# The MLP's first weights split in two by a casting DMA, a ScalarE negation and an accumulating DMA in ten chunks

## The chip, the core and the metric

The kernel runs on one core of one Trainium2 chip. The metric is the device time of one launch in microseconds, the median over timed runs. The engines are called PE (TensorE), DVE (VectorE), ACT (ScalarE), POOL (GpSimd) and SP (SyncE), as the profile does.

## What is computed

A decoder trunk of two layers on 1024 tokens of 1024 channels, all in float32. Layer 0 mixes tokens with a gated linear recurrence, layer 1 with causal windows; each mixer is followed by an MLP of 4096 hidden channels, and that MLP is where the change lies:

```python
def sq_relu_mlp(h, w1, w2):
    u = jax.nn.relu(jnp.einsum("bsd,df->bsf", h, w1))
    return jnp.einsum("bsf,fd->bsd", u * u, w2)

for i in range(DEPTH):
    ...
    h = modulate(rms_norm(x, norm_ffn_g[i]), sh_f, sc_f)
    x = x + gt_f[:, None, :] * sq_relu_mlp(h, ffn_w1[i], ffn_w2[i])
return rms_norm(x, final_norm_g)
```

The shifts, scales and gates (sh_f, sc_f, gt_f) come from the conditioning, a product of one vector with 12 matrices of 1024 x 1024.

## The kernel before

**Two parts of every operand.** PE multiplies float32r operands. To keep float32 accuracy each operand is held as two float32r parts, a high part (the value rounded) and a low part (what the rounding left). mm3 (lines 174 to 180) then issues three matmuls: high x high, high x low, low x high. A weight unit is loaded by SP as a raw float32 tile of 128 x 1024 (512 KB, load, line 97), then split_part (lines 168 to 172) makes the two parts of each half: ACT rounds the raw half into the high part, and DVE subtracts the high part from the raw half.

**The MLP** runs over eight chunks of 512 hidden channels. f1 makes a chunk's hidden channels: four units of w1 (128 hidden channels each), each used for both halves of the tokens, 24 matmuls per unit and half, so 192 matmuls. f2_fast then multiplies by w2 in four passes (r = 0 to 3), each of seven products (Winograd's form of Strassen's method, in the order 1, 5, 6, 3, 7, 2, 4) of six matmuls, so 168 matmuls. A chunk thus has 360 matmuls. In the program's rows the weights of a pass are four tiles: w_a11_a12 (products 1 and 2), w_a22_s1 (4 and 5), w_s2_s4 (3 and 6), w_s3 (7); the profile shortens them to w_a_a, w_a_s, w_s_s and w_s.

**After each product** of f2_fast the result is added into x. Products 5, 3, 2 and 4 are added by DVE straight from PSUM (line 770; 5 twice). Product 1 is copied by ACT (c1, line 789) and scaled by ACT; products 6 and 7 are added onto c1 by DVE (lines 800, 804), scaled by ACT (c, line 774) and added into x by POOL (line 779): one add for 1, one for 6, two for 7. Some of these adds go to the same blocks of x, so they are chained: DVE's add of product 3 waits for POOL's add of product 6, and DVE's add of product 4 for POOL's first add of product 7.

**What holds the order.** A tile framework arranges each engine's instructions into a fixed queue and puts in the semaphores. Three limits matter here. PE's results rotate through six PSUM banks, so a product can start only when the result six before it has been taken away. The split weights rotate through eight tiles of wpool; a unit of f1 takes two, a pass of f2_fast four, so the first two units of a chunk (u0, u1) take the tiles of pass 2 of the chunk before, and u2, u3 those of pass 3. Units are prepared one ahead (class Ahead, line 663). And the raw tiles (rawp, three buffers) serve w1, w2 and the 80 tiles of the conditioning's weights (mb, line 212), which are worked off by DVE (line 197, 1.2 us or more each), one per weight unit, during layer 0's MLP.

Of the kernel before, what the change touches and what calls it, by code (L numbers as in the profile page):

```python
# [10 lines left out]
F32 = mybir.dt.float32  # L11
# [4 lines left out]
P = 128  # L16
# [12 lines left out]
# Columns of the packed per-channel vectors, eight columns (one per block of channels) each.  # L29
# [13 lines left out]
def trunk_kernel(ctx, tc, xT, vecs, wmod, w_k, w_in, w_y, w_g, w_out, w_p, w1, w2, outT):  # L43
# [16 lines left out]
    class Blocks:  # L60
        """Eight blocks of channels of one half of the tokens, in two slots"""
# [41 lines left out]
    # The weights of the first products, in the order in which they are used: two blocks of rows  # L103
    # of six blocks of the input projection, and the conditioning's blocks of columns.
    mod_raw, k_raw = {}, []

    def piece(r, q, part):
        """Columns of a part of r, which is halved for the first two blocks of rows."""
        n = r.shape[-1] // (2 if q == 0 else 1)
        return part * n, part * n + n  # L110
# [29 lines left out]
    # silu(c) as a row on every partition  # L140
    cs = const.tile([P, NB], F32, name="cs")
    with tc.issue_after(S.activation(cs, vcol("c"), AF.Sigmoid).ins):
        # has the table of the first norm's square root loaded ahead of it
        S.activation(const.tile([P, 1], F32, name="early"), eps, AF.Sqrt)
# [3 lines left out]
    for n in range(2):  # L148
        ps = small_ps()
        # the columns of cs on diagonals, whose sums over the partitions are on every partition  # L150
# [9 lines left out]
    def split_unit(src, name, eng=None, drips=None):  # L160
        raw = load(src, name)
        drip(rate[0] if drips is None else drips)
        return [split_part(raw[:, c:c + H], f"{name}_{c}", eng) for c in (0, H)]

# [9 lines left out]
    def mm3(ps, unit, col, rh, rl, first, last):  # L174
        """ps += unit[:, col:col+128].T @ (rh + rl)"""
# [6 lines left out]
    def proj(unit, hh, hl):  # L182
        """One 128-row block of W.T @ h for one token half, K = 1024."""
# [11 lines left out]
    def mod_column(m, e, raw):  # L195
        """m[:, e] = raw @ cond"""
# [9 lines left out]
    def mod_steps():  # L206
        """The rest of the conditioning in small steps, taken between those of the other work."""
# [19 lines left out]
    def norm_scale(g, m, name):  # L227
        """g * (1 + scale)"""
# [5 lines left out]
    class SumSq:  # L234
        """Sums of squares of n tokens: up to three partial sums, added up by the tensor engine."""
# [19 lines left out]
    def rstd_bcast(ss, trace=None):  # L255
        """PSUM tile [P, n] with 1/sqrt(mean + eps) of every token on every partition."""
# [10 lines left out]
        # in two float32r parts on diagonals, whose sums over the partitions are on every partition  # L267
# [38 lines left out]
    # Six blocks of the input projection take the channels of the first half of the tokens  # L306
    # as the conditioning of each 128 of them is ready.
# [8 lines left out]
    def after(f, *args, **kw):  # L316
        """Issues behind what the last call on the same engine issued."""
# [7 lines left out]
    def column(dst, j, k, scale, first):  # L325
        """dst[:, k] = first + scale * (conditioning of channel block k)"""
# [16 lines left out]
    def prepare(q, part=0):  # L343
        """The float32r parts of the weights of two blocks of rows, or of one if q is 0"""
# [126 lines left out]
    # coefficient of the gate in log a: 8 * log_sigmoid(lambda)  # L471
# [17 lines left out]
    # log1p(z) = 2 s (1 + po)  # L489
# [11 lines left out]
    def gates(hd, unit, h):  # L501
        """RG-LRU of one head; its states take the place of its input."""
# [16 lines left out]
        for mi in range(2):  # L519
            b = 2 * hd + mi  # L520
            # a = exp(log a);  1 - a^2 = (1 + a^2) * tanh(-log a)
# [77 lines left out]
    # U[c]: the hidden channels of chunk c, in slots of two blocks each: (first or last two blocks,  # L599
    # half of the tokens), and the sums of them that the second product of the MLP takes  # L600
# [3 lines left out]
    def f1_block(unit, j, h, u, fast):  # L604
# [7 lines left out]
        def minus(a, n):  # L612
            """a less a block that is there in its two parts"""
# [15 lines left out]
        # for f2_fast the halves of the tokens change places  # L629
# [33 lines left out]
    class Ahead:  # L663
        """Units of weights, which are prepared one ahead of those in use"""
# [11 lines left out]
    # pieces of the conditioning by unit of a chunk of the MLP  # L676
    DRIPS = (1, 1, 1, 1, 1, 1, 1, 1)

    def f1_jobs(i, c, eng=None):
# [5 lines left out]
    def f1(i, c, halves, by_half=False, eng=None, side=iter(()), fast=False, ahead=None):  # L685
        """`side` is other work, a step of which is traced after each unit.

        `fast` is set where f2_fast takes the result: "in turn" if one half of the tokens is done before the other.
        """
# [22 lines left out]
    def f2_weights(i, c, r, eng=None):  # L712
        """The parts of blocks of rows r and r + 4 of W2.T for f2_fast, by the product that takes them"""
# [18 lines left out]
    def f2_weights_one(i, c, r, eng):  # L732
        """Those of f2_weights for the products that the first half of the tokens takes"""
# [12 lines left out]
    def f2_weights_two(i, c, r, eng):  # L746
        """The others"""
# [5 lines left out]
    def f2_fast(i, c, ahead, products=(1, 5, 6, 3, 7, 2, 4), side=iter(())):  # L753
        """The second product of the MLP by Winograd's form of Strassen's seven products.
# [358 lines left out]
```

## Time and profile before

| | |
|---|---|
| timed runs | 1795.46, 1798.42, 1798.61 us; median 1798.42 |
| span of the profiled execution | 1797.3 us (its own time is not listed beside the span; the median lies 1.1 us above it) |
| PE busy | 1718.5 us, 96% of the span |
| DVE busy | 1419.8 us, 79% |
| ACT busy | 913.7 us, 51% |
| POOL busy | 585.9 us, 33% |
| chain that ended last | PE 62%, DVE 22%, ACT 5%, issue 5%, DMA 4%, POOL 2% |

Busy time is an average over stages. The number to ask for in a stage is not who is busy but how long PE stands idle there, and which engine ends that idle time. In the stages of the change PE is almost never idle.

### The profile page before, as it was taken

The page shows a single profiled execution, that of the slowest core. Times are in us where ns is not written, and L with a number is a line of the kernel's source. Part 1 is how long each engine was busy: PE and PEld are TensorE (multiplying, and loading weights), DVE is VectorE, ACT ScalarE, POOL GpSimd, SP SyncE. Part 2 cuts the span into 40 slices and gives each one's busy share as a digit, 9 for nine tenths or more (in the row PEclk, how much of TensorE's full clock was granted, in tenths as well). Part 3 has the DMA queues.
Part 4 walks back from the last instruction along what each step waited for, and adds up shares of the span by engine and source line. Part 5 has one row for each costly group of instructions (what it writes and reads, how often), then busy time and mean ns, then how long its engine had stood idle before and what let it go on. Part 6 is the DMA issues. An engine that isn't in the chain of part 4 may idle for free.

```text
span 1797.3 us, 20872 instructions
## 1 busy us (share of the span) xinstructions
PE 1718.5 (96%) x7510; PEld 1405.2 (78%) x7510; DVE 1419.8 (79%) x2124; ACT 913.7 (51%) x1558; POOL 585.9 (33%) x434
## 2 busy tenths in 40 slices
PE   6899989989999999999999988999999999999997
PEld 4687768778788888888888766788887787878787
DVE  8997866678888889898876897958787878686836
ACT  4588884255454444545454464445444444545422
POOL 5323341242322414151324655511322324041403
PEclk8999989989999999999999988999999999999999
DMA  9223314521424233242213221231202111121202
GB/s 363 73 84 109 136 47 142 162 83 59 136 70 134 73 115 106 94 126 73 83 58 106 81 72 59 83 105 51 70 33 71 36 59 52 42 61 46 71 13 94
DMA packets 47479, 158.76 MB, mean 88 GB/s; under 512 B 5008, under 2 KB 7440, under 8 KB 47376
## 3 DMA queue, kind: packets, MB, share of 16 engines
q1 hardware_dynamic: 47376, 157.43, 26.9%
q8 instruction: 59, 0.97, 0.2%
q14 instruction: 44, 0.36, 0.1%
HBM read 153.21 MB, written 4.19 MB: 88 GB/s over the span
## 4 chain that ended last, share of the span: by engine, by line
PE 62%; DVE 22%; ACT 5%; issue 5%; DMA 4%; POOL 2%; DVEq 0%; SPq 0%; ACTq 0%; POOLq 0%
PE mm L178 20%; PE mm L179 20%; PE mm L180 20%; DMA mb<-in_wmod 3%; DVE mb L197 2%; DVE xa L770 1%; DVE mw L323 1%; POOL xa L779 1%; DVE pw L900 1%; DVE xb L770 1%; DVE xca L439 1%; PE sm L262 1%; DVE hl L291 1%; DVE w_a_s L171 1%; DVE xcb L439 1%
## 5 line engine op out<-in xcount | busy, mean ns | idle before, releaser
L178 PE MATMUL mm<-hh,w_w 128*128 128x512 f32 x1024 | 401.4, 392 | 0.9 <-DVE xa L770 0.9
L180 PE MATMUL mm<-hh,w_w 128*128 128x512 f32 x1024 | 400.9, 392 | 0.0
L179 PE MATMUL mm<-hl,w_w 128*128 128x512 f32 x1024 | 400.6, 391 | 0.0
L779 POOL TENSOR_TENSOR xb<-xb,c 128x512 f32<-128x512 f32 x104 | 150.4, 1446 | 632.1 <-ACT c L774 564.4
L178 PEld LDWEIGHTS mm<-hh,w_w 128*128 128x128 f32 x1024 | 193.5, 189 | 42.8 <-DVE xa L770 2.7
L180 PEld LDWEIGHTS mm<-hh,w_w 128*128 128x128 f32 x1024 | 193.6, 189 | 40.3
L179 PEld LDWEIGHTS mm<-hl,w_w 128*128 128x128 f32 x1024 | 193.5, 189 | 40.0
L779 POOL TENSOR_TENSOR xa<-xa,c 128x512 f32<-128x512 f32 x104 | 160.3, 1542 | 145.1 <-ACT c L774 145.1
L774 ACT ACTIVATE c<-c,mod 128x512 f32<-128x512 f32 x104 | 75.3, 724 | 209.7 <-DVE c L800 119.8
L197 DVE SCALAR_TENSOR_TENSOR mb<-mb,cond 128x1024 f32<-128x1024 f32 x80 | 113.8, 1423 | 55.2 <-DMA mb<-in_wmod 54.6
L620 ACT ACTIVATE relu<-mm 128x512 f32<-128x512 f32 x128 | 76.2, 595 | 152.4 <-PE mm L180 143.6
L170 ACT CAST w_w<-raw_w 128x512 fp32r<-128x512 f32 x192 | 113.5, 614 | 63.2 <-PE mm L180 50.6
L171 DVE TENSOR_TENSOR w_w<-raw_w,w_w 128x512 fp32r<-128x512 f32 x136 | 130.5, 967 | 16.8 <-ACT w_w L170 16.7
L770 DVE SCALAR_TENSOR_TENSOR xa<-mm,mod,xa 128x512 f32<-128x512 f32 x156 | 112.9, 741 | 16.6 <-POOL xa L779 16.6
L171 POOL TENSOR_TENSOR w_w<-raw_w,w_w 128x512 fp32r<-128x512 f32 x56 | 83.5, 1498 | 71.6 <-ACT w_w L170 62.6
L179 PE MATMUL mm<-u,w_w 128*128 128x512 f32 (+1 forms) x224 | 81.4, 363 | 1.7 <-DVE u L610 1.7
L178 PE MATMUL mm<-u,w_w 128*128 128x512 f32 (+1 forms) x224 | 80.8, 364 | 1.7 <-ACT u L609 1.7
L180 PE MATMUL mm<-u,w_w 128*128 128x512 f32 (+1 forms) x224 | 81.0, 362 | 0.0
L178 PE MATMUL mm<-u,w_a_a 128*128 128x512 f32 x200 | 79.1, 396 | 1.9 <-DVE xa L770 1.0
L610 DVE TENSOR_TENSOR u<-usq,u 128x512 fp32r<-128x512 f32 x102 | 72.9, 715 | 8.5 <-ACT u L609 7.5
L770 DVE SCALAR_TENSOR_TENSOR xb<-mm,mod,xb 128x512 f32<-128x512 f32 x104 | 77.0, 741 | 2.6 <-PE mm L180 2.2
L179 PE MATMUL mm<-u,w_a_a 128*128 128x512 f32 x200 | 78.0, 390 | 0.0
(332 smaller groups left out, 4078.3 us busy)
## 6 DMA issues: line engine op xcount, KB each, us to landing
raw_w<-in_w SPq DMA_DIRECT2D x148, 512.0 KB, 3.6
mb<-in_wmod SPq DMA_DIRECT2D x80, 512.0 KB, 3.6
mw<-in_wmod SPq DMA_DIRECT2D x16, 512.0 KB, 9.6
raw_in<-in_w_in SPq DMA_DIRECT2D x8, 512.0 KB, 3.7
raw_y<-in_w_y SPq DMA_DIRECT2D x8, 512.0 KB, 3.6
raw_o<-in_w_out SPq DMA_DIRECT2D x8, 512.0 KB, 3.7
outT<-o SPq DMA_DIRECT2D x12, 256.0 KB, 2.4
xa<-in_xT SPq DMA_DIRECT2D x4, 512.0 KB, 5.4
```

The lines of the kernel that those rows point to most:

```text
L170: S.copy(w[:, 0, 0:n], raw)
L171: (eng or V).tensor_sub(w[:, 1, 0:n], raw, w[:, 0, 0:n].bitcast(F32))
L178: PE.matmul(out=ps, lhsT=wh, rhs=rh, start=first, stop=False)
L179: PE.matmul(out=ps, lhsT=wh, rhs=rl, start=False, stop=False)
L180: PE.matmul(out=ps, lhsT=w[:, 1, c:c + P], rhs=rh, start=False, stop=last)
L197: V.scalar_tensor_tensor(raw, raw, 1.0, cond, op0=ALU.mult, op1=ALU.mult, accum_out=m[:, e:e + 1])
L439: V.scalar_tensor_tensor(o, xr[:, k:k + H], vcol(f"cw{k}", m), o, op0=ALU.mult, op1=ALU.add)
L610: eng.tensor_sub(u[n][:, 1, jj, :], src, u[n][:, 0, jj, :].bitcast(F32))
L620: S.activation(r, ps, AF.Relu)
L770: V.scalar_tensor_tensor(xb, ps, g[:, r + 4 * row:r + 4 * row + 1], xb, op0=ALU.mult, op1=ALU.add)
L774: S.activation(t, src, AF.Identity, scale=g[:, r + 4 * row:r + 4 * row + 1])
L779: G.tensor_add(xb, xb, t)
```

## The change

In chunks 1 to 5 of layer 0 and 2 to 6 of layer 1 (ten chunks, 40 units, 80 halves) split_unit is replaced by dma_unit. For each half POOL issues a DMA that reads w1 from HBM and writes it cast to float32r into the high part; ACT writes the negated high part into the low part; POOL issues a second DMA that reads the same half of w1 again and adds it onto the low part. No raw tile, no load on SP, no ACT cast and no DVE subtraction are left for these units. Comments and docstrings go too, which changes nothing but line numbers.

```diff
+    def dma_unit(src, name, drips):
+        unit = [split_tile(f"{name}_{c}") for c in (0, H)]
+        for w, c in zip(unit, (0, H)):
+            nc.gpsimd.dma_start(w[:, 0, :], src[:, c:c + H])
+        drip(drips)
+        for w, c in zip(unit, (0, H)):
+            S.activation(w[:, 1, :], w[:, 0, :].bitcast(F32), AF.Identity, scale=-1.0)
+            nc.gpsimd.dma_start(w[:, 1, :], src[:, c:c + H], accum_op=ALU.add)
+        return unit
...
-    def f1_jobs(i, c, eng=None):
+    def f1_jobs(i, c, eng=None, by_dma=False):
+        if by_dma and eng is None:
+            return [partial(lambda j: dma_unit(w1[i, c * 4 + j], f"w1_{i}_{c}_{j}", DRIPS[j]), j) for j in range(4)]
...
         for c in range(first, last):
-            yield from f1_jobs(i, c, G if (i, c) == (0, 0) else None)
+            yield from f1_jobs(i, c, G if (i, c) == (0, 0) else None, c > first)
             yield from f2_jobs(i, c)
```

The scheduler places the new instructions. On POOL, late in layer 1's chunk 4 (pass 2's adds, then pass 3's first), this stood there before: the two adds xb_1_84 and xa_1_82 with c_12090 are those of product 7 of pass 2.

```order
L779 TENSOR_TENSOR xb_0_83<-xb_0_83,c_12051 128x512
L779 TENSOR_TENSOR xa_0_81<-xa_0_81,c_12071 128x512
L779 TENSOR_TENSOR xb_1_84<-xb_1_84,c_12090 128x512
L779 TENSOR_TENSOR xa_1_82<-xa_1_82,c_12090 128x512
L779 TENSOR_TENSOR xb_0_83<-xb_0_83,c_12127 128x512
```

The same place on POOL now; w_w1_1_5_0_0 is the first half of u0 of chunk 5, w_w1_1_5_0_512 its second, w_w1_1_5_1_0 the first of u1, line 169 the casting DMA and line 173 the accumulating one.

```order
L792 TENSOR_TENSOR xb_0_83<-xb_0_83,c_12051 128x512
L169 DMA w_w1_1_5_0_0_12110<-in_w1 128x512
L792 TENSOR_TENSOR xa_0_81<-xa_0_81,c_12071 128x512
L169 DMA w_w1_1_5_0_512_12111<-in_w1 128x512
L169 DMA w_w1_1_5_1_0_12193<-in_w1 128x512
L173 DMA w_w1_1_5_0_0_12110<-in_w1 128x512
L792 TENSOR_TENSOR xb_1_84<-xb_1_84,c_12090 128x512
L792 TENSOR_TENSOR xa_1_82<-xa_1_82,c_12090 128x512
L173 DMA w_w1_1_5_0_512_12111<-in_w1 128x512
L169 DMA w_w1_1_5_1_512_12194<-in_w1 128x512
L173 DMA w_w1_1_5_1_0_12193<-in_w1 128x512
L792 TENSOR_TENSOR xb_0_83<-xb_0_83,c_12127 128x512
```

Four DMAs have come ahead of product 7's adds, three of them between them and product 6's. In layer 0 the accumulating DMA of u0's first half stands behind both adds of product 7 and not ahead of them; the rest is alike.

On DVE at the same place there stood, from the last weight tile of pass 3 on:

```order
L171 TENSOR_TENSOR w_s3_12039<-raw_w2_1_4_3_12024,w_s3_12039 128x256
L770 SCALAR_TENSOR_TENSOR xa_0_81<-mm_12054,mod1_5_6290,xa_0_81 128x512
L770 SCALAR_TENSOR_TENSOR xa_1_82<-mm_12054,mod1_5_6290,xa_1_82 128x512
L800 TENSOR_TENSOR c1_12049<-mm_12063,c1_12049 128x512
L171 TENSOR_TENSOR w_w1_1_5_0_0_12112<-raw_w1_1_5_0_12110,w_w1_1_5_0_0_12112 128x512
L770 SCALAR_TENSOR_TENSOR xa_0_81<-mm_12074,mod1_5_6290,xa_0_81 128x512
L804 TENSOR_TENSOR c1_12049<-mm_12082,c1_12049 128x512
L171 TENSOR_TENSOR w_w1_1_5_0_512_12115<-raw_w1_1_5_0_12110,w_w1_1_5_0_512_12115 128x512
```

and now stand:

```order
L182 TENSOR_TENSOR w_s3_12039<-raw_w2_1_4_3_12024,w_s3_12039 128x256
L732 TENSOR_TENSOR raw_w2_1_5_1_12511<-raw_w2_1_5_1_12511 128x256
L734 TENSOR_TENSOR raw_w2_1_5_1_12511<-raw_w2_1_5_1_12511 128x256
L783 SCALAR_TENSOR_TENSOR xa_0_81<-mm_12054,mod1_5_6292,xa_0_81 128x512
L783 SCALAR_TENSOR_TENSOR xa_1_82<-mm_12054,mod1_5_6292,xa_1_82 128x512
L813 TENSOR_TENSOR c1_12049<-mm_12063,c1_12049 128x512
L732 TENSOR_TENSOR raw_w2_1_5_2_12597<-raw_w2_1_5_2_12597 128x256
L734 TENSOR_TENSOR raw_w2_1_5_2_12597<-raw_w2_1_5_2_12597 128x256
L783 SCALAR_TENSOR_TENSOR xa_0_81<-mm_12074,mod1_5_6292,xa_0_81 128x512
L817 TENSOR_TENSOR c1_12049<-mm_12082,c1_12049 128x512
```

The subtractions of w1 are gone, and preparations of the next chunk's w2 (lines 732, 734; raw tiles are free earlier) have moved up ahead of pass 2's evictions.

On ACT at the same place there now stand, with line 172 the negation:

```order
L787 ACTIVATE c_12071<-c1_12049,mod1_5_6292 128x512
L172 ACTIVATE w_w1_1_5_0_0_12110<-w_w1_1_5_0_0_12110 128x512
L787 ACTIVATE c_12090<-c1_12049,mod1_5_6292 128x512
L172 ACTIVATE w_w1_1_5_0_512_12111<-w_w1_1_5_0_512_12111 128x512
L172 ACTIVATE w_w1_1_5_1_0_12193<-w_w1_1_5_1_0_12193 128x512
L802 COPY c1_12125<-mm_12118 128x512
L787 ACTIVATE c_12127<-mm_12118,mod1_5_6292 128x512
```

Before, casts of the same halves stood in about these places. A cast waited for a raw tile that had been loaded long before; a negation waits for a DMA that POOL has just issued, and the copy and the scaling of product 1 of pass 3, which free its PSUM bank, queue behind it.

## Rows read from the trace of the kernel before

**Rows 1.** The page, part 1: busy time, share, instructions.
```profile
PE 1718.5 (96%) x7510; PEld 1405.2 (78%) x7510; DVE 1419.8 (79%) x2124; ACT 913.7 (51%) x1558; POOL 585.9 (33%) x434
```

**Rows 2.** Windows over five chunks of each layer: PE, PEld, DVE, ACT, POOL busy.
```profile
466.37:877.38 411.01, 410.24 (x1800) 337.58 (x1801) 354.45 (x558) 199.03 (x350) 125.34 (x80) 1.00 0.32 102
1277.97:1694.09 416.12, 411.08 (x1802) 337.24 (x1800) 325.50 (x470) 197.56 (x350) 113.10 (x80) 1.00 0.16 51
```

**Rows 3.** Timeline of PE: first matmuls of chunks, and three late ones.
```profile
466.37 0.50 PE L178 MATMUL mm<-hh,w_w 128*128 128x512 f32 x1 [0.92 <-DVE xa L770]
...
713.40 0.50 PE L178 MATMUL mm<-hh,w_w 128*128 128x512 f32 x1
...
792.70 0.50 PE L178 MATMUL mm<-u,w_a_a 128*128 128x512 f32 x1
...
795.64 0.50 PE L178 MATMUL mm<-hh,w_w 128*128 128x512 f32 x1
...
877.38 0.39 PE L178 MATMUL mm<-hh,w_w 128*128 128x512 f32 x1
...
1444.42 0.39 PE L178 MATMUL mm<-hh,w_w 128*128 128x512 f32 x1
...
1520.66 0.50 PE L178 MATMUL mm<-ut,w_s_s 128*128 128x512 f32 x1 [0.96 <-DVE xa L770]
...
1527.63 0.39 PE L178 MATMUL mm<-hh,w_w 128*128 128x512 f32 x1
```

**Rows 4.** Page, part 5: the two groups of which 80 instructions each go.
```profile
L170 ACT CAST w_w<-raw_w 128x512 fp32r<-128x512 f32 x192 | 113.5, 614 | 63.2 <-PE mm L180 50.6
L171 DVE TENSOR_TENSOR w_w<-raw_w,w_w 128x512 fp32r<-128x512 f32 x136 | 130.5, 967 | 16.8 <-ACT w_w L170 16.7
```

**Rows 5.** DMA issues: KB each, median us to landing; SP's own row.
```profile
raw_w<-in_w SPq DMA_DIRECT2D x148, 512.0 KB, 3.6
...
outT<-o SPq DMA_DIRECT2D x12, 256.0 KB, 2.4
...
xb<-in_xT SPq DMA_DIRECT2D x4, 512.0 KB, 6.7
...
743.13 0.33 SPq L715 DMA_DIRECT2D raw_w<-in_w  x1
```

**Rows 6.** Timeline of POOL, layer 1's chunk 4.
```profile
1518.11 1.29 POOL L779 TENSOR_TENSOR xa<-xa,c 128x512 f32<-128x512 f32 x1 [3.10 <-ACT c L774]
1522.10 1.30 POOL L779 TENSOR_TENSOR xb<-xb,c 128x512 f32<-128x512 f32 x1 [2.70 <-ACT c L774]
1523.35 1.75 POOL L779 TENSOR_TENSOR xa<-xa,c 128x512 f32<-128x512 f32 x1
```

**Rows 7.** Timeline of DVE, layer 1's chunk 4.
```profile
1515.22 1.40 DVE L770 SCALAR_TENSOR_TENSOR xa<-mm,mod,xa 128x512 f32<-128x512 f32 x2
1516.54 0.68 DVE L800 TENSOR_TENSOR c<-mm,c 128x512 f32<-128x512 f32 x1
1518.57 1.37 DVE L171 TENSOR_TENSOR w_w<-raw_w,w_w 128x512 fp32r<-128x512 f32 x1 [1.36 <-ACT w_w L170]
1519.87 0.74 DVE L770 SCALAR_TENSOR_TENSOR xa<-mm,mod,xa 128x512 f32<-128x512 f32 x1
```

**Rows 8.** Timeline of ACT, layer 1's chunk 4: the scalings of products 6, 7.
```profile
1517.31 0.72 ACT L774 ACTIVATE c<-c,mod 128x512 f32<-128x512 f32 x1 [3.67 <-DVE c L800]
...
1521.30 0.72 ACT L774 ACTIVATE c<-c,mod 128x512 f32<-128x512 f32 x1 [1.72 <-DVE c L804]
```

**Rows 9.** Timeline of DVE, layer 0's chunk 4.
```profile
784.76 0.67 DVE L800 TENSOR_TENSOR c<-mm,c 128x512 f32<-128x512 f32 x1
...
789.65 2.32 DVE L197 SCALAR_TENSOR_TENSOR mb<-mb,cond 128x1024 f32<-128x1024 f32 x1
...
791.90 0.74 DVE L770 SCALAR_TENSOR_TENSOR xb<-mm,mod,xb 128x512 f32<-128x512 f32 x1
...
794.19 1.40 DVE L770 SCALAR_TENSOR_TENSOR xa<-mm,mod,xa 128x512 f32<-128x512 f32 x2
```

**Rows 10.** Timeline of POOL, layer 0's chunk 4.
```profile
786.34 1.29 POOL L779 TENSOR_TENSOR xa<-xa,c 128x512 f32<-128x512 f32 x1 [4.24 <-ACT c L774]
```

## The prediction

> **What bounds the kernel now.** I read the page's busy part first: PE is busy 96% of the span, DVE 79%, POOL 33% [rows 1]. A share over the whole span says nothing of a stage, so next come the windows over the two stretches in which the ten changed chunks lie. There PE is busy 410.24 of 411.01 us in layer 0 and 411.08 of 416.12 us in layer 1 [rows 2]; the granted clock is 1.00 in both, the upper of its two levels. The reader is to see that PE has almost nothing to give back. DVE, from which the change takes work, is busy 354.45 and 325.50 us there: loaded, but not the engine that sets the pace.
>
> The timeline of PE says how much there is to win. The chunk that begins at 795.64 ends at 877.38 without a gap: 81.74 us for 360 matmuls, 0.227 us each and 1.36 us for a product of six. Layer 0's chunk before it takes 795.64 - 713.40 = 82.24 us, so 0.5 us are idle; layer 1's takes 1527.63 - 1444.42 = 83.21 us, so 1.47 us are idle [rows 3]. The rows name the cause: PE waits for DVE's line 770, the instruction that takes a result out of a PSUM bank. The gaps lie late in f2_fast, where DVE runs behind, and are alike in four chunks of each layer; one of about 2 us stands before 466.37, none before layer 1's first changed chunk. Ceiling of any gain: 2 + 4 x 0.5 + 4 x 1.47 = about 10 us.
>
> **What goes.** 80 casts on ACT (0.614 us) and 80 subtractions on DVE (0.967 us) [rows 4], 49 us and 77 us of busy time, and 40 loads on SP. ACT gets 80 negations for its 80 casts, the same shape at the same 0.61 us, so nothing net. Of DVE's 77 us only what frees a bank earlier counts, at most the 10 us above. The order shows that it does not free it early: the subtractions stood after the addition of product 6 in pass 2, and that is the start of the chain on which PE waits, while two preparations of w2 now stand ahead of it.
>
> **What comes.** 160 DMAs on POOL, 16 in a chunk, which did not issue a DMA before. Two prices are unknown. **The issue**, time in which POOL does nothing else: SP's own row is 0.33 us, a POOL instruction of this width takes 1.29 us and up to 1.75 us beside DVE [rows 5, 6]. I take 1.3 us, because it is POOL that must write the transfer out; ends 0.33 and 1.75. **The landing**, from the start of the issue: 256 KB land in 2.4 us from SP, 512 KB in 3.6 us, and in 6.7 us when the queues are full [rows 5]. I take 3.6 us, since the accumulating transfer moves its 256 KB in twice; ends 2.4 and 6.7. Below nothing neither can be. The second reading of w1 adds 21 MB; the DMA share of these stretches is 0.32 and 0.16 [rows 2], so I cost that traffic at nothing, under cover of idle transfer engines; if they were full the landing would be that of the 6.7 us row.
>
> The Trainium skill, DMA: Bandwidth & Descriptors (Anatomy of one DMA, GpSimd path), gives a fixed 2.0 us plus the bytes over 436 GB/s, an estimate of 2.6 us for 256 KB. No row here shows a POOL transfer; by that figure the sum below would be 4.5 us instead of 6.5.
>
> **Layer 1, one chunk end (chunk 4 into 5).** Before, DVE evicts product 5 of pass 2 at 1515.22, adds product 6 at 1516.54 [rows 7], ACT scales it at 1517.31 [rows 8], POOL adds it at 1518.11 [rows 6], and DVE's eviction of product 3 at 1519.87 frees the bank for PE at 1520.66 [rows 3]. Now lines 732 and 734 stand ahead of 1515.22; they are half as wide as the addition of 0.68 us [rows 7], and I take 0.4 us each, so 0.8 us. The chain shifts: product 6's scaling ends near 1518.8, POOL's add runs 1518.8 to 1520.1, DVE follows at once (before, it stood 0.5 us behind a 1.37 us subtraction), PE resumes at 1521.0, 0.3 us late, and would reach product 2, three products on, at 1525.1.
>
> Then POOL: two casting issues and the accumulating one, 3 x 1.3 us, bring it to 1524.0. Its operand for product 7 is there by 1522.4 (0.74 + 0.67 us on DVE and 0.72 us on ACT behind 1520.1); before, POOL took it at 1522.10 [rows 6]. The add ends at 1525.3, DVE's eviction of product 4 of pass 2, chained to it (0.74 us), at 1526.1, and product 2 of pass 3, which needs that bank, starts 1.0 us late. f1 starts 0.3 + 1.0 = **1.3 us later** than before. ACT's negations wait for the landings at 1520.1 + 3.6 and 1521.4 + 3.6 us; behind them the scaling of product 1 of pass 3 ends at 1526.9, and its bank is wanted at 1527.5: hidden by 0.6 us. The low part of u0's second half lands at 1526.9 + 3.6 = 1530.5, wanted at 1532: hidden.
> Ends: issue 0.33, landing 2.4: +0.3 us. Issue 1.75: three issues more by 0.45, +2.7 us. Landing 6.7: the last negation ends at 1528.7, the bank comes at 1530.0, +3.8 us.
>
> **Layer 0, one chunk end (chunk 4 into 5).** A conditioning tile on DVE (mb) has moved behind product 6's addition, so that addition comes some 1.2 us before 784.76 [rows 9]. POOL: casting issue to 785.7 (its tile is free at about 784.4: 795.64 less the gap and eight products), product 6's add to 787.0 (before: 786.34 to 787.63 [rows 10]), two casting issues to 789.6, the adds of product 7 to 790.9 and 792.5. DVE evicts product 4 by 791.7; before, it began at 791.90 behind a 2.32 us mb [rows 9], and PE's product 2 started at 792.70 [rows 3]. Now it starts at 792.4: 0.3 us won. Behind an mb of 1.2 and a line 732 of 0.4 us product 5 of pass 3 is evicted by 794.7 (before by 794.19 + 1.40 [rows 9]), f1 could start at 795.25. But the low part of u0's first half is issued at 792.5 and lands at 796.1; f1's third matmul wants it at 795.7. **Net 0.0 us**: the new wait eats what DVE gives. Behind ACT's negations the bank of product 1 comes at 793.8, as wanted.
> Ends: both low: -0.4 us. Issue 1.75: the low part lands at 797.45, +1.4 us. Landing 6.7: ACT's queue holds product 1's bank to 796.9, +3.1 us.
>
> u1, u2 and u3 have 11, 22 and 33 us more, which cover them in all these cases. ACT's negations for u2 and u3 stand ahead of f1's first relu and can hold it some 7 us; six banks of 5.4 us each cover that, and ACT, busy half of these stretches [rows 2], catches up within f1.
>
> **Sum.** 5 x 0.0 + 5 x 1.3 = +6.5 us. The profiled span of 1797.3 us becomes 1803.8; the median of the runs stands 1.1 us above the span, so 1798.42 + 6.5 = 1805 us. Ends: issue and landing low, 5 x (-0.4) + 5 x 0.3 = -0.5 us; issue 1.75, 5 x 1.4 + 5 x 2.7 = +20.5 us; landing 6.7, 5 x 3.1 + 5 x 3.8 = +34.5 us.
>
> **Rivals.**
> *Faster.* DVE's relief frees banks before the new queue hurts: POOL's issues are as short as SP's row, and the preparations of w2 that moved up fall into time in which DVE would wait anyway (1.36 us of idle stands in rows 7). Then half of the 10 us comes back: 1793 us. For it: every gap is PE waiting on DVE. Against: the gap's chain runs through ACT and POOL, both made later. It decides at an issue below about 0.5 us.
> *Nothing.* Issue between, chain shifts and relief cancel: 1798 us. For it: the reserves found above are small in both directions.
> *Much slower.* The landing is nearer 6.7 us or the issue 1.75 us or more: 1819 to 1833 us. For the issue: POOL's add of 1.30 us at 1522.10 became 1.75 us at 1523.35 beside DVE's work [rows 6], and DVE is busy 78% to 86% of these stretches. For the landing: ACT, in order, holds PSUM banks while it waits, which the casts did not.
> The Trainium skill, SBUF — State Buffer (SBUF: two separate sides), says that a DMA issued from POOL cannot get its descriptors written while DVE runs a two-port operation. The adds and subtractions here have two inputs and are not of that kind, so the rule as written would not bite; no row here shows an issue beside DVE.
> That the DMAs are not issued as described can be ruled out: the order shows them on POOL.
>
> **Chances.** The runs lie within 3.2 us, so 0.2%, 3.6 us, is what a measurement can tell from no change. Forecast (a few us slower, 1802 to 1813) 0.40; much slower 0.21; nothing 0.24; faster 0.15. That gives slower 0.61, same 0.24, faster 0.15. The range must leave out no more than 2 in 10: 1795 (below it only the faster case) to 1832 (the landing's end); on the slow side alone it is 1802 to 1832.
>
> **What would show it.** Right: PE's idle time in layer 1's changed chunks grows from 1.47 to about 2.8 us and now stands before products 2 and 4 of pass 3; in layer 0 it sits on f1's third matmul, with a DMA as releaser; POOL's issues take about 1.3 us, the landing about 3.6. The first matmuls of f1 in the chunk rows shift accordingly. Wrong: no waits on DMA or ACT at the chunk ends (faster or nothing), waits of over 2 us there in every chunk (much slower), or PE waiting inside f1, for u1 to u3, which I have costed at nothing.

## The result and the profile after

The changed kernel takes 1810.9 us (median of 4 runs, 1808.15 to 1812.79) against 1798.35 us (4 runs): ratio 1.0074, 95% interval 1.0059 to 1.0089. It is 12.5 us slower. The forecast said 1805 us, a few us slower. The time came out near it; the place where the prediction put the loss did not.

The page's first part, which answers to [rows 1]: DVE is 79 us less busy, POOL 100 us more, and PE has as much to do as before.

```profile
PE 1717.6 (95%) x7510; PEld 1404.1 (78%) x7510; DVE 1340.9 (74%) x2044; ACT 916.8 (51%) x1558; POOL 685.7 (38%) x594
```

The windows over the five chunks of each layer answer to [rows 2] (from, to, length, then PE, PEld, DVE, ACT, POOL busy, granted clock, DMA share, GB/s).

```profile
468.63:892.31 423.68, 411.93 (x1802) 336.42 (x1800) 327.25 (x518) 200.29 (x351) 171.20 (x153) 1.00 0.46 121
1291.55:1705.63 414.08, 410.08 (x1802) 337.36 (x1800) 275.34 (x428) 199.79 (x351) 161.26 (x154) 1.00 0.33 75
```

Layer 0's five chunks went from 411.01 to 423.68 us: 12.7 us lost. Layer 1's went from 416.12 to 414.08 us: 2.0 us won. So the loss is all in layer 0, where 0.0 had been forecast, and none in layer 1, where 6.5 us had been. (The end of chunk 0, the first that the change touches, lies in front of the first window; its stops grew by another 1.3 us.) PE's timeline, which answers to [rows 3], shows the stops of layer 0's fourth chunk and of layer 1's.

```profile
792.19 0.47 PE L189 MATMUL mm<-ut,w_s_s 128*128 128x512 f32 x1 [0.67 <-DVE xa L783]
...
807.36 0.50 PE L189 MATMUL mm<-u,w_a_a 128*128 128x512 f32 x1 [1.31 <-DVE xb L783]
...
1534.40 0.50 PE L189 MATMUL mm<-ut,w_s_s 128*128 128x512 f32 x1 [1.18 <-DVE xa L783]
```

The first two are the stops of every chunk from the second to the fourth: some 0.85 us before product 6 of pass 2 (there was none before) and 1.47 us before product 2 of pass 3 (0.3 to 0.4 before). The first changed chunk has three, of 2.33, 1.71 and 1.47 us, worked out from the starts of neighbouring matmuls less the 0.227 us of one. The third row, in layer 1, stood there before at 1.12 us and is 1.33 us now; in the last two chunks it is 0.36 us. All of these wait for DVE's line 783 (770 before), an eviction. One more, of 0.73 us in the first changed chunk, waits for a sum of hidden channels; no stop above 0.3 us in the two windows waits for a DMA.

What DVE does in layer 0 at these two stops (timeline of DVE, then of POOL):

```profile
788.88 1.23 DVE L208 SCALAR_TENSOR_TENSOR mb<-mb,cond 128x1024 f32<-128x1024 f32 x1
...
791.29 0.75 DVE L783 SCALAR_TENSOR_TENSOR xa<-mm,mod,xa 128x512 f32<-128x512 f32 x1 [1.18 <-POOL xa L792]
...
803.27 3.36 DVE L208 SCALAR_TENSOR_TENSOR mb<-mb,cond 128x1024 f32<-128x1024 f32 x1
...
806.56 0.74 DVE L783 SCALAR_TENSOR_TENSOR xb<-mm,mod,xb 128x512 f32<-128x512 f32 x1
```

```profile
789.00 2.26 POOL L792 TENSOR_TENSOR xa<-xa,c 128x512 f32<-128x512 f32 x1 [5.78 <-ACT c L787]
...
801.85 1.13 POOL L169 DMA_DIRECT2D w_w<-in_w  x2
802.99 1.31 POOL L792 TENSOR_TENSOR xb<-xb,c 128x512 f32<-128x512 f32 x1
804.24 1.29 POOL L792 TENSOR_TENSOR xa<-xa,c 128x512 f32<-128x512 f32 x1
```

Both are a conditioning tile (mb) beside an add of POOL. At 788.88 the mb runs on and POOL's add takes 2.26 us instead of 1.29; the eviction chained to that add starts late. At 803.27 POOL's two adds of product 7 run on (1.31 and 1.29 us) and the mb takes 3.36 us instead of 1.21: POOL's second add ends at 805.53, and 805.53 + 1.21 = 806.74 is about where the mb ends. The eviction of product 4 stands behind it, and PE behind that. Before, one mb stood at this chunk end beside the adds, with 2.32 us [rows 9], and none in pass 1.

By these rows the mutual delay is enough for both stops, as an estimate: with an add of 1.29 us the first eviction would have followed at 790.3 and not at 791.29, 1.0 us earlier for a stop of 0.82; with an mb of 1.21 us the second would have begun at 804.5 and not at 806.56, 2.1 us earlier for a stop of 1.47.

POOL's issues have a part in it too. Product 7's operand was ready at 801.46 + 0.72 = 802.18:

```profile
801.46 0.72 ACT L787 ACTIVATE c<-c,mod 128x512 f32<-128x512 f32 x1 [1.02 <-DVE c L817]
```

The two casting issues kept POOL until 802.98, so both adds ran 0.8 us later, and the mb that waited for them with them.

The Trainium skill, SBUF — State Buffer (Who interferes with whom), says that VectorE and GpSimd share one pair of ports, and that an operation with two SBUF inputs and a GpSimd operation that reads SBUF exclude each other for a whole instruction. These rows agree, both ways round: the mb of 788.88 came first, ends at 790.11, and 790.11 + 1.29 = 791.40 is about where POOL's add ends (791.26); the mb of 803.27 came second.

The prices that had been bounded (page, part 5, and part 6; the rows of lines 169 and 173 by themselves, in ns):

```profile
L172 ACT ACTIVATE w_w<-w_w 128x512 fp32r<-128x512 f32 x80 | 50.4, 631 | 151.1 <-DMA w_w<-in_w 141.1
L173 POOL DMA_DIRECT2D w_w<-in_w x80 | 77.1, 1010 | 92.5 <-ACT w_w L172 87.0
...
w_w<-in_w POOLq DMA_DIRECT2D x160, 256.0 KB, 4.7
```

```profile
L169 POOL DMA_DIRECT2D w_w<-in_w x80: 535/810/1242, 454.4 to 1635.3; - x80
...
DMA to landing us min/median/max: 2.8/4.6/8.6
...
L173 POOL DMA_DIRECT2D w_w<-in_w x80: 851/921/1522, 460.5 to 1642.8; - x80
...
DMA to landing us min/median/max: 3.6/5.1/9.1
```

An issue takes 0.81 us in the median for the casting transfer and 0.92 us for the accumulating one, and they overlap (two casting ones back to back: 1.13 us); 1.3 us had been assumed. The landing takes 4.6 and 5.1 us; 3.6 had been assumed. ACT stands 141 us waiting for castings. By the figure that the prediction quoted from the Trainium skill, DMA: Bandwidth & Descriptors (Anatomy of one DMA, GpSimd path), the landing would have been an estimated 2.6 us; even the shortest one here is 2.8.

So two theories went to the chip. **Conditioning theory:** freed raw tiles let the scheduler move mb tiles in among layer 0's evictions; POOL's issues and ACT's waits cost nothing. **Queue theory**, the prediction's: issues and waits ahead of product 7's adds cost it.

### The profile page after: what moved, and what is told of

Read it like the earlier page. It is cut to its first block, busy times and chain, and to the rows that moved or that the text cites. A ratio compares the mean times of both kernels' runs of the same rounds, so it can differ in the third digit from the quotient of the medians.

```text
span 1809.1 us, 21134 instructions
## 1 busy us (share of the span) xinstructions
PE 1717.6 (95%) x7510; PEld 1404.1 (78%) x7510; DVE 1340.9 (74%) x2044; ACT 916.8 (51%) x1558; POOL 685.7 (38%) x594
## 4 chain that ended last, share of the span: by engine, by line
PE 46%; DVE 24%; DMA 9%; ACT 8%; issue 8%; POOL 6%; DVEq 0%; SPq 0%; ACTq 0%; POOLq 0%
PE mm L189 15%; PE mm L190 15%; PE mm L191 15%; DMA mb<-in_wmod 3%; DMA w_w<-in_w 3%; POOL xa L792 2%; DVE mb L208 2%; DMA raw_w<-in_w 2%; POOL xb L792 2%; DVE mw L334 1%; DVE xa L783 1%; DVE pw L913 1%; DVE w_a_s L182 1%; DVE xb L783 1%; POOL w_w L169 1%
## 5 line engine op out<-in xcount | busy, mean ns | idle before, releaser
L191 PE MATMUL mm<-hh,w_w 128*128 128x512 f32 x1024 | 400.3, 391 | 0.1
L191 PEld LDWEIGHTS mm<-hh,w_w 128*128 128x128 f32 x1024 | 193.2, 189 | 41.4 <-DMA w_w<-in_w 1.2
L172 ACT ACTIVATE w_w<-w_w 128x512 fp32r<-128x512 f32 x80 | 50.4, 631 | 151.1 <-DMA w_w<-in_w 141.1
L173 POOL DMA_DIRECT2D w_w<-in_w x80 | 77.1, 1010 | 92.5 <-ACT w_w L172 87.0
L181 ACT CAST w_w<-raw_w 128x512 fp32r<-128x512 f32 x112 | 67.5, 615 | 54.4 <-PE mm L191 49.3
L182 DVE TENSOR_TENSOR w_a_a<-raw_w,w_a_a 128x512 fp32r<-128x512 f32 x48 | 37.3, 777 | 72.1 <-ACT w_a_a L181 72.0
L189 PE MATMUL mm<-u,w_a_a 128*128 128x512 f32 x200 | 79.0, 395 | 10.5 <-DVE xb L783 7.2
L191 PE MATMUL mm<-u,w_w 128*128 128x512 f32 (+1 forms) x224 | 81.2, 363 | 0.0
```

The source lines that it names most:

```text
L172: S.activation(w[:, 1, :], w[:, 0, :].bitcast(F32), AF.Identity, scale=-1.0)
L173: nc.gpsimd.dma_start(w[:, 1, :], src[:, c:c + H], accum_op=ALU.add)
L181: S.copy(w[:, 0, 0:n], raw)
L182: (eng or V).tensor_sub(w[:, 1, 0:n], raw, w[:, 0, 0:n].bitcast(F32))
L189: PE.matmul(out=ps, lhsT=wh, rhs=rh, start=first, stop=False)
L191: PE.matmul(out=ps, lhsT=w[:, 1, c:c + P], rhs=rh, start=False, stop=last)
```

## The experiments

Each median stands beside a ratio to the kernel before on the same chip (1797.7 to 1798.4 us), with its 95% interval. "Layer 0" and "layer 1" are the lengths of the five-chunk stretches in each trace, from the first matmul of the first changed chunk's f1 to that of the chunk behind the last.

| | median us | ratio (interval) | layer 0 | layer 1 |
|---|---|---|---|---|
| before | 1798.4 | 1 | 411.0 | 416.1 |
| after | 1810.9 | 1.0074 (1.0059 to 1.0089) | 423.7 | 414.1 |
| l1_only | 1792.3 | 0.9969 (0.9956 to 0.9981) | 410.6 | 412.6 |
| l0_only | 1812.9 | 1.0085 (1.0071 to 1.0099) | 423.5 | 416.2 |
| after_mb_held | 1828.4 | 1.0173 (1.0159 to 1.0187) | 449.4 | - |
| before_mb_held | 1806.7 | 1.0054 (1.0042 to 1.0067) | 424.0 | - |
| after_no_mb | 1783.1 | 0.9925 (0.9913 to 0.9937) | 411.2 | 411.1 |
| before_no_mb | 1792.8 | 0.9973 (0.9963 to 0.9983) | 416.1 | 416.2 |
| after_two_casts | 1809.4 | 1.0064 (1.0052 to 1.0076) | 423.3 | - |
| l1_prep_held | 1791.7 | 0.9974 (0.9964 to 0.9984) | - | 410.5 |
| after_mb_spread | 1861.1 | 1.0357 (1.0343 to 1.0372) | 473.4 | - |
| before_mb_spread | 1812.5 | 1.0077 (1.0065 to 1.0090) | 426.3 | - |
| after_mb_psum | 1807.9 | 1.0051 (1.0037 to 1.0065) | 421.3 | - |
| before_mb_psum | 1793.6 | 0.9977 (0.9968 to 0.9986) | 408.1 | - |

### Where the loss is: l1_only and l0_only

```diff
-            yield from f1_jobs(i, c, G if (i, c) == (0, 0) else None, c > first)
+            yield from f1_jobs(i, c, G if (i, c) == (0, 0) else None, c > first and i == 1)
```

(i == 0 in the other.)

> The ten chunks' new way is kept in layer 1's five chunks alone; layer 0's chunks split their weights as before. Two theories. Conditioning theory: with the raw tiles freed, the scheduler moves conditioning tiles (mb) on DVE in among the evictions of layer 0's passes, and POOL's issues and ACT's waits cost nothing; layer 1 has no mb, so it is about neutral: by the chunk starts of the two traces layer 1 gains 13.58 - 11.54 = 2.0 us, so 1796.3 us. Queue theory (the prediction's): POOL's issues ahead of product 7's adds and ACT's waits cost 1.3 us per chunk of layer 1: 1805 us.

> The new way in layer 0's five chunks alone. By the chunk starts of the two traces layer 0 loses 892.31 - 877.38 = 14.9 us, of which 1.0 us was there before the first changed weight: 1812 to 1813 us by both theories; by the prediction's own terms for layer 0 (0.0 us a chunk) 1798 us.

Measured: 1792.3 and 1812.9 us, 5.5 us below and 15.1 us above the kernel before. The queue theory's 1805 for layer 1 falls, and so does the prediction's 0.0 a chunk for layer 0. Layer 1's chunks alone beat both kernels. Of the 5.5 us the trace shows 3.6 in the stretch of layer 1's chunks; its first changed chunk starts 2.9 us earlier than in the trace of before, and already 3.3 us earlier at a place in layer 0 that the two programs share, so that part is one execution against another.

### With no conditioning: after_no_mb and before_no_mb

```diff
             for e in range(NB):
+                if i == 1:
+                    yield
+                    continue
                 raw = rawp.tile([P, D + 256], F32, tag="raw", name=f"mb{i}_{j}_{e}")[:, 0:D]
```

(and a memset of m to zero for i == 1)

> The changed kernel without the conditioning of layer 1: its 48 tiles (mb) are neither loaded nor reduced, the shifts, scales and gates of layer 1 are zeros; all of layer 0's changed chunks are then free of mb, as layer 1's are. Conditioning theory: DMAs, issues and waits on POOL and ACT cost layer 0 nothing, its five chunks become as in layer 1 (at most those of the control), and the whole is 3 to 6 us below the control before_no_mb. Queue theory: 1.2 us a chunk and 2.3 us at the first end are left in layer 0, less the 2 to 5 us that layer 1 gains: 3 to 6 us above the control.

> The kernel before with the same conditioning left out, as the control. Layer 0's gaps before (0.3 to 0.5 us a chunk) are those of product 2 behind an mb; they may go or become layer 1's 1.3 us: 1795 to 1802 us by both theories.

Both kernels leave out layer 1's conditioning, and so the mb of layer 0's changed chunks. Measured: 1783.1 against 1792.8 us. Without mb the same change is worth 9.7 us (1792.77 - 1783.06); with mb it costs 12.5. The windows, after_no_mb first, then the control:

```profile
454.52:865.73 411.21, 409.01 (x1801) 337.52 (x1800) 275.16 (x428) 200.06 (x351) 162.00 (x153) 1.00 0.32 76
1265.51:1676.58 411.07, 408.94 (x1801) 337.60 (x1800) 275.17 (x428) 199.94 (x351) 162.15 (x154) 1.00 0.33 76
```

```profile
455.50:871.62 416.12, 411.05 (x1801) 337.06 (x1800) 325.76 (x470) 196.25 (x348) 112.25 (x80) 1.00 0.16 50
```

Layer 0 is now like layer 1, with PE idle for 2.2 us in five chunks; in the control it is idle for 5.1 us, as layer 1 was in [rows 2]. POOL still issues all its DMAs (162.0 us busy, as in layer 1 of after), and ACT still waits 147 us for castings. The loss needs the conditioning: that is shown. It does not yet show what of the conditioning does it, since its loads, its raw tiles and its instructions went together. The two stretches are 4.9 and 5.1 us shorter than the control's (416.1 and 416.2), and that is the 9.7 us. One thing limits this: the control's layer 0 is itself 5.1 us longer than that of the kernel before (411.0), with a stop of 1.15 us before product 6 in every chunk as in layer 1. So what the change gains there is about what leaving out the mb had lost; why it lost it was not followed.

### ACT's waits alone: after_two_casts

```diff
-            S.activation(w[:, 1, :], w[:, 0, :].bitcast(F32), AF.Identity, scale=-1.0)
-            nc.gpsimd.dma_start(w[:, 1, :], src[:, c:c + H], accum_op=ALU.add)
+            nc.gpsimd.dma_start(w[:, 1, :], src[:, c:c + H])
```

> The changed kernel with the negation left out and a plain casting DMA in place of the accumulating one, so that the low part holds a second copy of the high part: as many POOL issues, but ACT never waits for a DMA and POOL never for ACT's negation. DVE's order, with its mb tiles, stays that of the change. Conditioning theory: no change, 1809 to 1812 us. Queue theory, in so far as ACT's waits (141 us in the trace of after) hold scalings and bank releases: the 1.47 us before product 2 of pass 3 shrink towards 0.3, 1803 to 1806 us.

Measured: 1809.4 us, no gain that the intervals can tell. ACT no longer waits for any casting, and yet PE's stop before product 2 has grown to 2.2 us. On DVE and PE, at the same chunk end:

```profile
800.62 4.10 DVE L207 SCALAR_TENSOR_TENSOR mb<-mb,cond 128x1024 f32<-128x1024 f32 x1
...
804.66 0.74 DVE L782 SCALAR_TENSOR_TENSOR xb<-mm,mod,xb 128x512 f32<-128x512 f32 x1
```

```profile
805.46 0.50 PE L188 MATMUL mm<-u,w_a_a 128*128 128x512 f32 x1 [2.05 <-DVE xb L782]
```

The mb between the evictions takes 4.10 us. POOL's two adds beside it end at 802.88, and 802.88 + 1.21 = 804.09, so some 0.6 us of it, in which POOL issues DMAs, stays unexplained:

```profile
801.58 1.30 POOL L791 TENSOR_TENSOR xa<-xa,c 128x512 f32<-128x512 f32 x1
```

So the run took ACT's waits away and got a longer mb, and does not show that these waits are free. In the trace of after they are hidden, but only just. At the fourth chunk's end:

```profile
806.44 1.24 ACT L172 ACTIVATE w_w<-w_w 128x512 fp32r<-128x512 f32 x2 [3.73 <-DMA w_w<-in_w]
...
808.05 0.69 ACT L787 ACTIVATE c<-mm,mod 128x512 f32<-128x512 f32 x1
```

```profile
808.86 0.43 PE L189 MATMUL mm<-ut,w_a_s 128*128 128x512 f32 x1
```

ACT's scaling frees the bank of product 1 of pass 3 at 808.74, and product 4, which takes this bank, starts at 808.86. Without the stop of 1.47 us it would have wanted the bank at 807.4, an estimate, and waited some 1.4 us for ACT. Two waits end almost together here, and taking away one of them leaves the other.

### Moving the conditioning: four misses

after_mb_held and before_mb_held take the tiles in f1, all behind the last eviction of the f2_fast before; after_mb_spread and before_mb_spread take three there, three behind unit 0 and two behind unit 1.

```diff
-                mod_column(m, e, raw)
+                with tc.issue_after(hold[0]) if hold else nullcontext():
+                    mod_column(m, e, raw)
...
-    DRIPS = (1, 1, 1, 1, 1, 1, 1, 1)
+    DRIPS = (0, 2, 3, 3, 0, 0, 0, 0)
...
             next(side, None)
+        hold[:] = [last_traced(V)]
```

(In the spread version DRIPS is (0, 3, 3, 2, 0, 0, 0, 0), and hold is set again after each unit of f1.)

> The changed kernel, with the conditioning tiles of layer 0's chunks taken in f1 (none, two, three and three with its four units) and held on DVE behind the last eviction of the f2_fast before, so that none stands among the evictions. Conditioning theory: the gaps of 0.85 us before product 6 of pass 2 and of 1.47 us before product 2 of pass 3 go, and so do the 2.33 and 1.71 us of the first changed chunk: layer 0's five chunks take 410 us as before, and the time is 1798 us or some us below. Queue theory: the 1.47 us before product 2 of pass 3 stay, since POOL issues two DMAs ahead of product 7's adds; 4 x 1.2 us and the first end's 2.3 us are left, 1805 us.

> The kernel before with the same conditioning schedule and hold, as the control. Both theories: at most the gaps of layer 0 (2 us before the first changed chunk and four of 0.3 to 0.5 us) can go, 1795 to 1798 us.

> The changed kernel, complete, with the conditioning tiles of a chunk (three, three and two) taken with f1's second, third and fourth unit and held on DVE behind the last instruction traced before: the first three behind f2_fast's last eviction, the others behind the squares of units 0 and 1. after_mb_held had all eight at the head of f1, where the later ones waited up to 3.1 us for their loads and made f2_fast's sums late. Conditioning theory: no mb stands among the evictions and DVE has room in f1 (22.5 of 43.5 us busy without mb), so layer 0's five chunks end without the 0.85 and 1.47 us gaps: 1785 to 1790 us, below the kernel before and below layer 1's chunks alone (1792.3). Queue theory: 1.2 us a chunk stay, 1795 us or more. If DVE has no room in f1 after all, f2_fast's first product with a sum waits, as in after_mb_held.

> The kernel before with the same spread, as the control. Its 40 subtractions of layer 0 stay among the evictions and in f1: by before_mb_held its chunk ends keep gaps of 2 us, and the time is 1796 to 1802 us; the DMA way gains over it what it gained without mb, some 8 to 10 us.

Measured: 1828.4 and 1806.7 us, 1861.1 and 1812.5 us. All four are slower than before, and both theories had the controls wrong. The stop before product 2 did shrink (to between nothing and 0.57 us in after_mb_held), but a larger one came at the head of f2_fast, where PE waits for a sum of hidden channels (5.0 us in the second changed chunk of after_mb_held, below; 8.6 us in the third of after_mb_spread). First PE and DVE in after_mb_held, then ACT in after_mb_spread:

```profile
600.12 0.79 PE L189 MATMUL mm<-ut,w_s_s 128*128 128x512 f32 x1 [4.87 <-ACT ut L623]
```

```profile
565.58 1.23 DVE L208 SCALAR_TENSOR_TENSOR mb<-mb,cond 128x1024 f32<-128x1024 f32 x1 [2.89 <-DMA mb<-in_wmod]
```

```profile
676.66 0.63 ACT L172 ACTIVATE w_w<-w_w 128x512 fp32r<-128x512 f32 x1 [9.17 <-DMA w_w<-in_w]
...
690.00 0.62 ACT L181 CAST w_a_a<-raw_w 128x512 fp32r<-128x512 f32 x1 [7.81 <-DMA raw_w<-in_w]
...
693.20 0.62 ACT L623 CAST ut<-usq 128x512 fp32r<-128x512 f32 x1 [0.39 <-DVE usq L651]
```

In after_mb_held DVE waits for the loads of five mb, 7.3 us in all, with f1's further work on DVE queued behind them. In after_mb_spread ACT stands 9.17 us for a casting DMA, ahead of f1's first relu, and 7.81 us for a raw tile of w2, ahead of f1's squares. Each of these makes f2_fast's sums late; how much each adds to the stops was not followed. So these runs replaced one wait by others and do not decide between the theories, except that the place of mb is not free in either kernel.

### Contention or place: after_mb_psum and before_mb_psum

```diff
+        if cond_ps:
+            r3 = raw.rearrange("p (q t) -> p q t", q=2)
+            V.scalar_tensor_tensor(r3, r3, 1.0, cond_ps[0][:, None, :].to_broadcast([P, 2, H]),
+                                   op0=ALU.mult, op1=ALU.mult, accum_out=m[:, e:e + 1])
+            return
...
+    cond_ps.append(small_ps())
+    S.copy(cond_ps[0], cond[:, 0:H])
     for c in range(1, 6):
```

> The changed kernel; in layer 0's changed chunks the conditioning tiles (mb) multiply by a copy of the conditioning's first half that lies in a PSUM bank, used for both halves of the tile (so layer 1's shifts, scales and gates come from half the vector): the same loads, the same instruction over 128x1024, as many mb among the evictions of a chunk end (one of them stands one place earlier), but one operand fewer from SBUF. The conditioning theory has two readings. Contention: mb costs what it does because POOL's adds and an mb with both operands in SBUF hold each other up (3.36 us instead of 1.21 where it lies under product 7's two adds); then mb takes some 1.3 us everywhere, POOL's adds 1.3, the gaps of 0.85 and 1.47 us shrink to a few tenths, and the time is 1796 to 1801 us. Place: mb costs by standing ahead of an eviction, 1.2 us each time; then the gaps stay near 1 us each and the time is 1806 to 1811 us.

> The kernel before with the same copy in PSUM, as the control: its one stretched mb of a chunk (2.32 us) gets shorter, and of its gaps of 0.3 to 0.5 us at most all goes: 1795 to 1798 us by both readings.

Measured: 1807.9 us and 1793.6 us. The control first: its groups of mb (with the vector in PSUM, and in SBUF), one of them between POOL's adds, and the window of its layer 0.

```profile
L201 DVE SCALAR_TENSOR_TENSOR mb<-mb,sm 128x1024 f32<-128x1024 f32 x40 | 48.6, 1216 | 21.1 <-DMA mb<-in_wmod 20.8 <-DVE w_w L171 0.3
...
L204 DVE SCALAR_TENSOR_TENSOR mb<-mb,cond 128x1024 f32<-128x1024 f32 x40 | 56.9, 1423 | 31.3 <-DMA mb<-in_wmod 31.2
```

```profile
785.17 1.21 DVE L201 SCALAR_TENSOR_TENSOR mb<-mb,sm 128x1024 f32<-128x1024 f32 x1
```

```profile
464.09:872.22 408.13, 408.13 (x1802) 337.94 (x1801) 350.10 (x558) 199.55 (x351) 112.80 (x80) 1.00 0.32 104
```

With one operand in PSUM an mb takes 1.22 us wherever it stands, and PE does not stop once in five chunks. So in the kernel before, layer 0's gaps were contention. (This profiled execution, 1789.0 us, is the shortest of eleven; the median lies 4.7 us above it. The five chunks are 2.9 us shorter than before, the median 4.4 us.)

In after_mb_psum the mb take 1.216 us too, and the stops of 0.85 and 1.47 us are gone from the second to the fourth chunk (the first still has 2.21 and 0.82 us before the same products). In their place, in each of the first four chunk ends, stands one of 1.3 to 2.5 us before product 4 of pass 3. Its profiled execution (1802.7 us) is the shortest of six; their median lies 5 us above it. POOL, ACT and PE at the fourth chunk's end, and the window around it:

```profile
796.51 0.57 POOL L169 DMA_DIRECT2D w_w<-in_w  x1
```

```profile
802.15 0.63 ACT L172 ACTIVATE w_w<-w_w 128x512 fp32r<-128x512 f32 x1 [4.18 <-DMA w_w<-in_w]
802.68 0.57 ACT L809 COPY c<-mm 128x512 f32<-128x512 f32 x1
```

```profile
803.89 0.50 PE L189 MATMUL mm<-ut,w_a_s 128*128 128x512 f32 x1 [1.55 <-ACT c L794]
```

```profile
796.00:803.00 7.00, 6.34 (x28) 4.68 (x26) 5.78 (x10) 2.62 (x5) 5.95 (x7) 1.00 0.93 293
```

The third casting DMA is issued at 796.51 and its negation starts at 802.15, 5.6 us later; the transfer engines are 93% busy in these 7 us. Behind the negation, in ACT's queue, wait the copy and the scaling of product 1 of pass 3, and PE waits for that bank. This is the queue theory's wait, in the place and by the chain that the prediction's "landing" end describes. So neither reading holds alone. The time lies in the range of the place reading (1806 to 1811 us), but the rows show the contention gone and another wait in its place. Contention is real and removable, but in the changed kernel a second wait stands right behind it: taking away ACT's wait (after_two_casts) leaves the mb's, taking away the contention leaves ACT's.

### A last step in layer 1: l1_prep_held

```diff
-        E.tensor_sub(s3, a11, a21)
-        s1 = a21
-        E.tensor_add(s1, a21, a22)
+        s1 = a21
+        with tc.issue_after(hold[0]) if hold else nullcontext():
+            E.tensor_sub(s3, a11, a21)
+            E.tensor_add(s1, a21, a22)
```

(hold is the last eviction of the f2_fast before; layer 1's chunks alone take the DMA way.)

> The version of layer 1's chunks alone (1792.3 us), with the first two steps of w2's preparation held on DVE behind the last eviction of the f2_fast before, so that the pair that waits for its raw tile's load no longer stands between product 6's addition and the eviction of product 3. If that pair (eviction 0.67 us behind POOL's add in the trace of after) sets the gap that is left in layer 1's chunks, it shrinks from about 1.3 to 0.6 us or less and the time falls by 2 to 4 us, to 1789 us. If POOL's chain sets it, nothing changes: 1792 us.

Measured: 1791.7 us; against l1_only's 1792.3 the intervals overlap. In the trace the stretch is 2.1 us shorter (410.5 against 412.6) and its largest stop is 0.7 us. That shows no gain: in traces of the unheld version of layer 1's chunks the stretch takes from 409.4 us (after_mb_psum) over 411.1 (after_no_mb) to 414.1 us (after). That the pair sets part of the gap is therefore not shown by a time or by the stretch.

## Why the prediction was right and where it was not

**The sign and the size** came out: slower, 1810.9 us, inside the forecast's 1802 to 1813. That was luck. The sum behind it, 5 x 0.0 + 5 x 1.3 = 6.5 us, was half of the 12.5 us measured, and both of its terms were wrong, in opposite directions: by the timed runs with one layer alone they are about +15 us for layer 0 and -5.5 us for layer 1 (these do not quite add up to 12.5). The prediction's own signs were against it as well: no large stop at a chunk end waits for a DMA or for ACT, and PE's idle time in layer 1's chunks fell, by the windows from 5.0 to 4.0 us.

**Layer 0, net 0.0.** This is the step that failed. It had product 4 evicted right behind POOL's first add of product 7, as if the mb ahead of that eviction were done in its 1.2 us meanwhile; it took 3.36, and [rows 9] had shown 2.32 us for an mb beside POOL's adds. The adds themselves it had placed well, the two casting issues ahead of them included: their ends, 804.30 and 805.53, lie at 790.8 and 792.1 when the traces are laid together at product 2 of pass 2 (785.61 before, 799.08 now), against 790.9 and 792.5. It looked at one chunk end's last products only: pass 1, where another mb had come beside POOL's add of product 6, cost 0.85 us more, and the first changed chunk's three stops of 5.5 us together were not looked at. The low part of u0's first half as the new wait was seen, but at 0.2 us and in two chunks (an L191 matmul).

**Layer 1, +1.3 a chunk.** The term was over-sized in its issue price. Chunk 4 into 5 on POOL, to be held against [rows 6]:

```profile
1531.66 1.28 POOL L792 TENSOR_TENSOR xa<-xa,c 128x512 f32<-128x512 f32 x1 [3.37 <-ACT c L787]
1532.90 1.11 POOL L169 DMA_DIRECT2D w_w<-in_w  x2
1533.99 0.93 POOL L173 DMA_DIRECT2D w_w<-in_w  x1
1535.85 1.29 POOL L792 TENSOR_TENSOR xb<-xb,c 128x512 f32<-128x512 f32 x1 [0.93 <-ACT c L787]
```

The three issues take 2.0 us, not 3.9, and POOL then still waits 0.93 us for product 7's operand. The 1.0 us is hidden. The 0.3 us from w2's preparations was near in size, PE's stop before product 6 going from 1.12 to 1.33 us in this chunk, but not in kind. Product 6's add on POOL did not come 0.7 us later: measured from the first matmul of the chunk (1444.42 and 1458.11), it came at 73.7 and 73.6 us. It was a second pair of preparations, which waited for its load, that put the eviction of product 3 0.67 us behind the end of POOL's add (0.47 before):

```profile
1532.50 0.73 DVE L732 TENSOR_TENSOR raw_w<-raw_w 128x256 f32<-128x256 f32 x1 [1.75 <-DMA raw_w<-in_w]
...
1533.61 0.74 DVE L783 SCALAR_TENSOR_TENSOR xa<-mm,mod,xa 128x512 f32<-128x512 f32 x1
```

Why the stop is only 0.36 us in the last two chunks was not followed.

**Costed at nothing.** u1 to u3, the delay of f1's first relu and ACT's cast for negation cost nothing in the changed kernel, as said. The second reading of w1 "under cover of idle transfer engines" held in layer 1; in layer 0's chunk ends the cover was thin (0.74 busy from 797 to 810 us in the trace of after, 0.93 in after_mb_psum), and the landings there reached over 8 us.

**The rivals.** "Faster" was right for layer 1; without layer 1's conditioning the change gains 9.7 us over its control in both layers together. "Much slower" had the landing's mechanism right, and after_mb_psum shows it, but in the changed kernel it lies behind the mb.

**Still open:** how the loss of layer 0 divides between the mb's place, its contention, POOL's two issues ahead of product 7's adds and the transfers that its loads slow down; no run took the issues away, and no complete kernel took away both waits at once. The conditioning's vector in PSUM together with the DMA way in layer 1 alone was not tried; before_mb_psum is faster than before, but uses half of the vector.

## What to carry to other kernels

Taking work off an engine also frees the buffers that this work held, and whatever else draws on them is then scheduled elsewhere: read from the order where all of it went, in every pass and in the first changed iteration, and not only where the removed instructions stood. Price an instruction by its row in the company that it will have (an mb is 1.21 us alone and 3.36 us under two POOL adds). Before removing a wait, look for the one that ends just behind it. And try a change stage by stage: here one layer alone is 5.5 us faster while both together are 12.5 us slower.

## What the runs showed of the hardware that was not expected

An instruction of DVE with both inputs in SBUF can lose to two POOL adds in a row: the mb at 803.27 did not get in between the add that ended at 804.30 and the one that ran from 804.24. With one input in PSUM the same instruction took 1.21 us between and beside such adds.

After a stop of 4.9 us in after_mb_held PE resumed at the lower of its two clocks: granted 0.50 (1.2 GHz) for the next 6.2 us, in which matmuls, from 602.07 on, started 0.43 us apart, not 0.227. The windows of the stop and behind it:

```profile
595.00:599.90 4.90, 0.25 (x2) 0.00 (x0) 4.68 (x8) 4.00 (x8) 0.00 (x0) 0.98 0.00 2
600.12:606.30 6.18, 5.62 (x12) 4.09 (x13) 5.50 (x11) 4.51 (x9) 0.60 (x1) 0.50 0.12 36
```

So a stop of this length cost more than itself.
